# Strassen's scheme for groups 3 and 4 of three gate/up stages and four chunks of three down stages, with 1024-wide weight splits in gate/up

## The chip, the core and the metric

The kernel runs on one core of a Trainium2 chip, in one launch. The metric is the device time of that launch in microseconds (us), as a median of several executions. The core's engines are TensorE (matmuls into PSUM, which has 8 banks of 128 x 512 f32), VectorE, ScalarE and GpSimd for elementwise work, and SyncE (SP), from whose queue all loads and stores of this kernel are issued. Each engine runs its instructions in the order in which the program lists them, and waits on semaphores for what others have made.

## The reference

Two layers over 256 tokens of 1024 features, all in f32. Each layer is an FFN with a half step, a mixer (attention with a memory group), and a second FFN with a half step:

```python
def swiglu(h, w_gate, w_up, w_down):
    return (jax.nn.silu(h @ w_gate) * (h @ w_up)) @ w_down

for i in range(DEPTH):                                   # DEPTH = 2
    h = rmsnorm(x, ffn1_norm[i])
    x = x + 0.5 * swiglu(h, ffn1_w_gate[i], ffn1_w_up[i], ffn1_w_down[i])
    ...                                                  # mixer: x = x + concat(self_out, mem_out) @ W_out
    h = rmsnorm(x, ffn2_norm[i])
    x = x + 0.5 * swiglu(h, ffn2_w_gate[i], ffn2_w_up[i], ffn2_w_down[i])
```

`w_gate` and `w_up` are 1024 x 2816, `w_down` is 2816 x 1024. There are four FFNs: (0, 1), (0, 2), (1, 1) and (1, 2), by layer and place in the layer. The change touches the last three, and the width of the weight splits in all four.

## The kernel before

**Products.** An f32 product is made of three matmuls on values rounded to a shorter f32 form: with `hi` the rounded value and `lo` the rest, `dense` (L409) issues x_hi·w_hi (L416), x_hi·w_lo (L419) and x_lo·w_hi (L422) into the same bank. One `dense` multiplies a 128 x 128 block of activations by a 128 x 512 block of weights. Here it is called a product, and a product is three matmuls.

**Weights** come in chunks of four 128 x 512 blocks (1 MB). `loader` (L272) fetches a chunk into one of three `raw` tiles (NRAW); `split_hi` (L305) casts it to `hi` on ScalarE (L321), one instruction for each 512 columns; `split_lo` (L324) forms `lo` = raw - hi on VectorE (L340). `hi` and `lo` live in four tile pairs (NHL). A raw tile is free again once its splits are made, and a hi/lo pair once the products on it have run (`uses`). The three are "idle" threads of a planner.

**The planner.** The class `Flow` (L47) walks through the kernel with assumed durations and lists each engine's instructions in the order that its clock gives; the chip then runs them in that order, at its own speed. `dense` advances TensorE's clock and waits until its operands are due. Evacuations, sums and the like are threads that `yield` the time or the condition they wait for. Splits are put in order when the engine has at most 0.4 us of work before it, or when the chunk is the one that TensorE is at.

**A gate/up stage** (L640) has 11 groups of 256 columns of `w_gate` and the same 256 of `w_up`; a group has two chunks (upper and lower half of the 1024 rows), 8 products each: two token blocks `tb` times four row blocks. A group's two banks `gu` are evacuated by `evac` (L517): silu on ScalarE (L526), product with the up half on VectorE (L529), a block transpose (L537), then through DRAM (`hd`, `hr`, L543 and L548) to turn the blocks, and a split into `ht` (L557, L559), which the down stage takes as its stationary operand. Before the `ht` split is put in order, the thread waits 4.0 us of the planner's clock for the load of `hr`.

**A down stage** (L667) has 11 chunks, one for each group, accumulating in four `acc` banks. Chunks 0 to 7 run one after the other; chunks 8, 9 and 10 run together, ordered by token block and half, so that `finish` (L493) can add one quarter of the result to x while the next is computed. `finish` also transposes x for the next stage (`prep_half`, L450).

**Seven products for eight.** Three chunks of each down stage but the first (`SEVEN`, L362) already use Strassen's scheme (in Winograd's form): a chunk is a 2 x 2 grid of blocks and so is its activation operand; sums of blocks are formed on both sides and seven products take the place of eight. `split_lo` forms four sums of weights (`wsum`, L334), `seven_forms` (L564) four sums of activations from `hr`, `seven` (L591) issues the products, four of them into banks `m` of their own, and `seven_sums` (L602) adds these to x after the last such chunk: eight VectorE operations, which alternate with other work. Such a chunk needs two hi/lo pairs for its seven blocks. The forms of the third such chunk wait until the down stage has reached the second (`prog`).

Of the kernel before, what the change touches and what calls it, by code (L numbers as in the profile page):

```python
# [142 lines left out]
def kernel(  # L143
# [96 lines left out]
    class Chunk:  # L240
        def __init__(self, parts):
            self.parts = parts
            self.raw = self.hi = self.lo = None
            self.arrive = self.early = None
            self.seven = False
            self.hit = [None] * 7
            self.lot = [None] * 7
            self.tt = [None] * 4
            self.uses = 0

        def part(self, lo, q):

            t = (self.lo if lo else self.hi)
            if self.seven:
                t, q = t[q // 4], q % 4
            return t[:, q * 512:(q + 1) * 512]

    chunks = []
# [6 lines left out]
    def add_chunk(parts, uses=8):  # L265
        c = Chunk(parts)
        c.uses = uses
        c.index = len(chunks)
        chunks.append(c)
        return c  # L270

    def loader():  # L272
        for i, c in enumerate(chunks):
# [3 lines left out]
            c.block = lambda q, c=c: c.raw[:, q * 512:(q + 1) * 512] if not c.seven else c.raw[:, (0, 2, 3)[q] * 512:  # L277
                                                                                          (1, 3, 4)[q] * 512]
# [26 lines left out]
    def split_hi():  # L305
        for i, c in enumerate(chunks):
            n = 2 if c.seven else 1
            yield lambda: c.raw is not None and hl_left[0] >= n
            hl_left[0] -= n
            yield c.early or c.arrive  # L310
            c.hi, c.lo = ([whl.tile([P, 2048], F32R, tag=x, name=f"{x}{i}_{j}") for j in range(n)] for x in ("hi", "lo"))
            if not c.seven:
                c.hi, c.lo = c.hi[0], c.lo[0]
            for q in range(7 if c.seven else 4):
                if q == 2:
                    yield c.arrive
                if c.seven and q >= 3:
                    yield lambda: c.tt[q - 3] is not None
                    yield c.tt[q - 3]
                yield calm_a(i)  # L320
                nc.scalar.copy(out=c.part(0, q), in_=c.block(q))  # L321
                c.hit[q] = flow.act(512)

    def split_lo():  # L324
        for i, c in enumerate(chunks):
# [18 lines left out]
            if c.seven:  # L344
                g2.give(4)
# [1152 lines left out]
```

## Time and profile before

| | |
|---|---|
| median of three runs | 965.41 us (964.82 to 967.43) |
| the profiled execution's own time | 964.95 us |
| its span, first to last instruction | 963.2 us |
| TensorE matmuls, instructions | 4525 |
| VectorE instructions | 1569 |
| ScalarE instructions | 1215 |
| moved by DMA | 204.04 MB, mean 212 GB/s |

The span is what the profile shows; the 1.75 us between it and the execution's time lie before the first and after the last instruction. A page of the profile gives, in this order, the busy time of each engine, the same in 40 slices of the span, the DMA queues, the chain of work that ended last, and the costliest groups of instructions. PE is TensorE's matmuls and PEld its weight loads, DVE is VectorE, ACT is ScalarE, POOL is GpSimd. A group is named by its line, engine and operation, then by what it writes and reads in the program's names (`lo<-raw,hi`), shape, and count.

The four gate/up stages begin at 9.0, 317.5, 496.9 and 781.2 us, their down stages at 130.6, 437.7, 617.1 and 901.4 us.

### The profile page before, as it was taken

To read this page: it belongs to the slowest core of one execution; us is meant where nothing else is said; L and a number is where in the kernel's file an instruction comes from. 1 tells how busy PE (TensorE), PEld (TensorE's weight loads), DVE (VectorE), ACT (ScalarE), POOL (GpSimd) and SP (SyncE) were. 2 spreads that over 40 slices of the span, in tenths; PEclk is the share of its full clock that TensorE was granted. 3 is DMA by queue.
4 is the path that set the end of the run, shared out by engine and by line. 5 is a ranking of instruction groups with operands and counts; after the bars stand their busy time and mean duration, and the time that the engine had idled before them with its cause. 6 is when DMAs were issued, how large, how long until landed. Compare 5 with 4: busy or idle time off the path is not lost.

```text
span 963.2 us, 13464 instructions
## 1 busy us (share of the span) xinstructions
PE 954.8 (99%) x4525; PEld 783.9 (81%) x4525; DVE 745.0 (77%) x1569; ACT 567.9 (59%) x1215; POOL 60.5 (6%) x65
## 2 busy tenths in 40 slices
PE   8999999999999999999999999999999999999998
PEld 7888888888777888888888888888787788888886
DVE  6777777788777877759986775797989886776785
ACT  6655555666676655545645555565677765554551
POOL 0000000021210000000000000000343100000000
PEclk9999999999999999999999999999999999999999
DMA  8988877486525479766568777666641468777661
GB/s 282 328 267 285 250 263 246 145 272 208 176 88 175 154 224 284 235 229 205 184 208 254 247 245 220 212 202 219 207 143 44 134 196 283 232 254 225 215 190 44
DMA packets 169295, 204.04 MB, mean 212 GB/s; under 512 B 9673, under 2 KB 144394, under 8 KB 169226
## 3 DMA queue, kind: packets, MB, share of 16 engines
q1 hardware_dynamic: 169226, 203.18, 66.0%
q8 instruction: 35, 0.57, 0.2%
q14 instruction: 34, 0.28, 0.1%
HBM read 188.99 MB, written 14.16 MB: 211 GB/s over the span
## 4 chain that ended last, share of the span: by engine, by line
PE 94%; DVE 3%; ACT 1%; DMA 1%; SPq 0%; issue 0%; ACTq 0%
PE gu L422 17%; PE gu L416 17%; PE gu L419 17%; PE acc L416 9%; PE acc L422 9%; PE acc L419 9%; PE pj L422 3%; PE pj L416 3%; PE pj L419 3%; PE xtp L429 1%; PE ptp L429 1%; PE S L1139 1%; PE AV L1220 1%; PE m L422 1%; PE m L419 1%; PE m L416 1%
## 5 line engine op out<-in xcount | busy, mean ns | idle before, releaser
L340 DVE TENSOR_TENSOR lo<-raw,hi 128x512 fp32r<-128x512 f32 x647 | 413.7, 684 | 103.9 <-ACT hi L321 100.0
L321 ACT CAST hi<-raw 128x512 fp32r<-128x512 f32 x647 | 361.7, 618 | 219.0 <-PE gu L422 123.6
L422 PE MATMUL gu<-hi,xl 128*128 128x512 f32 x704 | 274.3, 390 | 0.0
L416 PE MATMUL gu<-hi,xh 128*128 128x512 f32 x704 | 274.1, 389 | 0.0
L419 PE MATMUL gu<-lo,xh 128*128 128x512 f32 x704 | 274.0, 389 | 0.0
L422 PEld LDWEIGHTS gu<-hi,xl 128*128 128x128 f32 x704 | 132.2, 188 | 27.4
L419 PEld LDWEIGHTS gu<-lo,xh 128*128 128x128 f32 x704 | 132.2, 188 | 27.3
L416 PEld LDWEIGHTS gu<-hi,xh 128*128 128x128 f32 x704 | 132.2, 188 | 27.3
L416 PE MATMUL acc<-hi,ht 128*128 128x512 f32 x280 | 109.6, 391 | 0.0
L422 PE MATMUL acc<-hi,ht 128*128 128x512 f32 x280 | 109.2, 390 | 0.0
L419 PE MATMUL acc<-lo,ht 128*128 128x512 f32 x280 | 109.1, 390 | 0.0
L422 PE MATMUL pj<-hi,xl 128*128 128x512 f32 x160 | 64.5, 403 | 0.0
L419 PE MATMUL pj<-lo,xh 128*128 128x512 f32 x160 | 63.6, 397 | 0.0
L416 PE MATMUL pj<-hi,xh 128*128 128x512 f32 x160 | 63.5, 397 | 0.0
L422 PEld LDWEIGHTS acc<-hi,ht 128*128 128x128 f32 x280 | 52.6, 188 | 11.0
L419 PEld LDWEIGHTS acc<-lo,ht 128*128 128x128 f32 x280 | 52.6, 188 | 10.7
L416 PEld LDWEIGHTS acc<-hi,ht 128*128 128x128 f32 x280 | 52.6, 188 | 10.7
L526 ACT ACTIVATE sil<-gu,xr 128x256 f32<-128x256 f32 x88 | 41.5, 472 | 28.6 <-PE gu L422 28.6
L559 DVE TENSOR_TENSOR ht<-hr,ht 128x512 fp32r<-128x512 f32 x35 | 24.1, 687 | 32.2 <-ACT ht L557 32.2
L529 DVE SCALAR_TENSOR_TENSOR h<-gu,xr,sil 128x256 f32<-128x256 f32 x88 | 42.2, 479 | 5.8 <-ACT sil L526 4.5
L557 ACT CAST ht<-hr 128x512 fp32r<-128x512 f32 x35 | 21.6, 618 | 41.9 <-DMA hr<-hd 41.8
L436 POOL TENSOR_TENSOR xr<-v,nhalf 128x1 f32<-128x1 f32 x12 | 8.4, 698 | 502.3 <-DVE v L434 502.3
(191 smaller groups left out, 1069.0 us busy)
## 6 DMA issues: line engine op xcount, KB each, us to landing
raw<-in_ffn_w_down_dram SPq DMA_DIRECT2D x176, 256.0 KB, 4.1
raw<-in_ffn_w_gate_dram SPq DMA_DIRECT2D x86, 512.0 KB, 4.3
raw<-in_ffn_w_up_dram SPq DMA_DIRECT2D x86, 512.0 KB, 5.5
raw<-in_w_in_dram SPq DMA_DIRECT2D x32, 512.0 KB, 4.1
hd<-hb SPq DMA_DIRECT2D x44, 256.0 KB, 2.3
hr<-hd SPq DMA_DIRECT2D x44, 256.0 KB, 5.3
raw<-in_w_out_dram SPq DMA_DIRECT2D x8, 1024.0 KB, 5.0
raw<-in_w_mem_kv_dram SPq DMA_DIRECT2D x4, 1024.0 KB, 5.4
```

The source lines that it names most:

```text
L321: nc.scalar.copy(out=c.part(0, q), in_=c.block(q))
L340: nc.vector.tensor_sub(c.part(1, q), c.block(q), c.part(0, q).bitcast(F32))
L416: nc.tensor.matmul(out=ps, lhsT=xh, rhs=wh, start=start, stop=False)
L419: nc.tensor.matmul(out=ps, lhsT=xh, rhs=wl, start=False, stop=False)
L422: nc.tensor.matmul(out=ps, lhsT=xl, rhs=wh, start=False, stop=stop)
L429: nc.tensor.transpose(out=dst, in_=src, identity=flip if flipped else ident)
L526: nc.scalar.activation(sil, ps[tb][:, 0:256], AF.Silu, scale=xt.r[tb])
L529: nc.vector.scalar_tensor_tensor(out=h, in0=ps[tb][:, 256:512], scalar=xt.r[tb], in1=sil, op0=ALU.mult, op1=ALU.mult)
L557: nc.scalar.copy(out=hi, in_=src)
L559: nc.vector.tensor_sub(lo, src, hi.bitcast(F32))
L1139: nc.tensor.matmul(out=ss[e][:, pr, :nk], lhsT=q[rows, pr, :], rhs=k[rows, pr, :], start=i == 0, stop=i == len(passes) - 1)
L1220: nc.tensor.matmul(out=av[64 * e:64 * e + 64, pr, :], lhsT=vsrc(kb, pr, e), rhs=pts[e][:, pr, kb, :], start=(kb == 0), stop=(kb == nb - 1))
```

## The change

1. In the last three FFNs, gate/up groups 3 and 4 are computed together. Their four chunks are a 2 x 2 grid of weights (row halves by groups), x is a 2 x 2 grid of activations (token blocks by row halves). `pair_items` forms four sums of weights (t1 to t4, four VectorE operations of 512 each), `pair_forms` four sums of x (eight VectorE operations, four casts), `product` issues seven products m1 to m7 of four `dense` each into a bank each, and `pair_sums` adds them to the four results, which `evac` then takes from SBUF. Blocks 11, 12, 22, 21 of the weights are loaded once; three of them (b11, b22, b21) are also used plainly. The seven items stand between plain chunks of groups 5 to 8, after groups 0 to 2.
2. Splits work on items with their own list of sources, no longer on chunks. A plain gate/up chunk is split by two instructions of 1024 columns on each engine instead of four of 512 (all four FFNs, the first two chunks of the kernel excepted).
3. `SEVEN` now has chunks 1, 3, 5 and 7 in each of the last three down stages.
4. `evac` waits 6.5 us of the planner's clock for `hr` instead of 4.0.
5. The forms of x need the f32 values `y` of the normalised, transposed x; `prep_half` keeps these four tiles until `pair_forms` has used them.

```diff
+    class Item:
+        def __init__(self, raws, uses=8, w=1):
+            self.raws, self.uses = raws, uses
...
+            self.n, self.frees, self.takes, self.gives = 1, 1, 0, 0
+            self.sums, self.t = [], []
+            self.index = len(items)
+            w = 1 if len(items) < 2 else w
+            self.units = [(self.own(q, w), q, w, None) for q in range(0, 4, w)]
+            items.append(self)
...
     def split_hi():
-        for i, c in enumerate(chunks):
-            n = 2 if c.seven else 1
-            yield lambda: c.raw is not None and hl_left[0] >= n
+        for i, it in enumerate(items):
+            yield lambda: hl_left[0] >= it.n and all(r.raw is not None for r in it.raws)
+            hl_left[0] -= it.n
+            yield max(r.early or r.arrive for r in it.raws)
...
+            for src, q, w, dep in it.units:
...
+                if dep is not None:
+                    yield lambda: it.st[dep] is not None
+                    yield it.st[dep]
                 yield calm_a(i)
-                nc.scalar.copy(out=c.part(0, q), in_=c.block(q))
+                nc.scalar.copy(out=it.part(0, q, w), in_=src())
...
     def split_lo():
+        for i, it in enumerate(items):
+            if it.sums:
+                yield lambda: all(r.raw is not None for r in it.raws) and g2.left >= it.takes + 2
+                yield max(r.arrive for r in it.raws)
+                it.t += [g2.take([P, 512], F32, "wsum") for _ in range(it.takes)]
+                for j, (x, y) in enumerate(it.sums):
+                    yield calm_v(i)
+                    nc.vector.tensor_sub(it.t[j], x(), y())
+                    it.st[j] = flow.dve(512)
+            for src, q, w, dep in it.units:
+                yield lambda: it.hit[q] is not None
+                yield it.hit[q]
+                yield calm_v(i)
+                nc.vector.tensor_sub(it.part(1, q, w), src(), it.part(0, q, w).bitcast(F32))
...
+            raw_left[0] += it.frees
+            g2.give(it.gives)
...
-    SEVEN = {(0, 1): (), (0, 2): (1, 4, 6), (1, 1): (1, 4, 6), (1, 2): (1, 4, 7)}
+    SEVEN = {(0, 1): (), (0, 2): (1, 3, 5, 7), (1, 1): (1, 3, 5, 7), (1, 2): (1, 3, 5, 7)}
+    PAIR = {(0, 1): None, (0, 2): 3, (1, 1): 3, (1, 2): 3}
...
+    def pair_items(raws):
+        r11, r12, r22, r21 = raws
+        def sums(need, x, y, held=None):
+            it = Item(need, 4)
+            it.t, it.takes = (held.t, 0) if held else ([], 4)
...
+            it.sums = [(at_(x, j), at_(y, j)) for j in range(4)]
+            it.units = [((lambda j=j: it.t[j]), j, 1, j) for j in range(4)]
+            return it
+        def plain(r, frees):
+            it = Item([r], 4, 2)
+            it.frees = frees
+            return it
...
+        def m5():
+            made["t1"] = sums([r12, r11], 0, 1)
+        def m7():
+            made["t3"] = sums([r22, r12], 0, 1)
+            made["t3"].gives = 4
+        def m6():
+            made["t2"] = sums([r22], 0, made["t1"], made["t1"])
+            made["t2"].frees = 0
...
+        def m4():
+            made["t4"] = sums([r21], 0, made["t2"], made["t2"])
+            made["t4"].gives = 4
...
     def plan_ffn(l, nm, wg, wu, wd):
+        work = [(g, c) for g in range(NG) for c in range(2)]
+        if pair is not None:
+            rest = [w for w in work if w[0] not in (pair, pair + 1)]
+            n = 2 * pair
+            p = iter(rest[n:])
+            work = rest[:n]
...
+            for x in ("11", "m1", "p", "12", "m5", "p", "22", "m7", "p", "m6", "p", "m3", "p", "p", "21", "m2", "p", "m4"):
+                work.append(next(p) if x == "p" else x)
+            work += list(p)
...
             hr = g2.take([P, 4, P], F32, "hr")
             nc.sync.dma_start(out=hr, in_=hd.rearrange("a i b x -> (i b) a x"))
-            yield flow.now + 4.0
+            yield flow.now + 6.5
...
+        def pair_forms():
+            yield lambda: len(xt.y) == 4 and g4.left >= 4
+            y = xt.y
+            fm = [g4.take([P, 2, 4, P], F32R, "xf") for _ in range(4)]
...
+            for j, o in ((0, (1, 1)), (2, (1, 0)), (1, (0, 0)), (3, (0, 1))):
+                yield lambda: flow.free["A"] <= flow.now + SLACK
+                nc.scalar.copy(out=fm[j][:, 0], in_=y[o])
+                yield flow.act(512)
+                yield lambda: flow.free["V"] <= flow.now + SLACK
+                nc.vector.tensor_sub(fm[j][:, 1], y[o], fm[j].bitcast(F32)[:, 0])
+                xt.ft[j] = flow.dve(512)
+                g2.give()
...
+        def pair_sums():
...
+            yield lambda: "m1" in mt
+            yield mt["m1"]
+            yield g2.has()
+            u = g2.take([P, 512], F32, "gu_u")
+            nc.scalar.copy(out=u, in_=pb["m1"])
...
+            yield lambda: "m6" in mt and "m7" in mt
+            yield mt["m6"]
+            yield g2.has(3)
+            u2, w, v = (g2.take([P, 512], F32, "gu_v") for _ in range(3))
+            plus(u2, u, pb["m6"])
+            plus(w, u2, pb["m5"])
+            t = plus(v, w, pb["m7"])
+            plus(u2, u2, pb["m7"])
...
+            for m, (g, tb), x in (("m3", (1, 0), w), ("m2", (0, 0), u), ("m4", (0, 1), u2)):
+                yield lambda: m in mt
+                yield mt[m]
+                t = plus(x, x, pb[m])
...
+        def product(m):
...
+            flow.until(banks.has())
+            pb[m] = bank("pair_" + m, (P, 512))
+            if m == "m1":
+                flow.spawn(pair_sums())
+                for e in range(2):
+                    flow.spawn(evac(pair + e, pps[e], pend[e], (g2, g2)))
+            for k in range(4):
...
+                t = dense(pb[m], fh, fl, ready, pit[name], k, k == 0, k == 3)
+            mt[m] = t
```

222 lines of the change are left out of this document (136 added, 86 removed).

## The prediction

> **What bounds the kernel now.** I read the page first, then TensorE's own waits, then the busy time of each engine in each stage. The page:
>
> ```profile
> span 963.2 us, 13464 instructions
> PE 954.8 (99%) x4525; PEld 783.9 (81%) x4525; DVE 745.0 (77%) x1569; ACT 567.9 (59%) x1215; POOL 60.5 (6%) x65
> ...
> PE   8999999999999999999999999999999999999998
> PEclk9999999999999999999999999999999999999999
> ...
> PE 94%; DVE 3%; ACT 1%; DMA 1%; SPq 0%; issue 0%; ACTq 0%
> ```
>
> TensorE is busy 99%, at full granted clock in every slice, and 94% of the chain that ended last is its work. Busy alone would not prove a bound, so its waits come next:
>
> ```profile
> PE warm L1425 <- POOL ident masks.py:199: 1.4, 1, 1.4
> PE xtp L429 <- DMA x<-in_x_dram: 1.1, 2, 0.9
> PE ptp L429 <- DVE pe L1266: 0.7, 2, 0.6
> PE acc L416 <- DVE oT L1127: 0.4, 1, 0.4
> PE qktp L429 <- DVE m L1045: 0.4, 1, 0.4
> PE qktp L429 <- ACT PT L1153: 0.4, 1, 0.4
> ```
>
> These six rows are the whole view (what waited for what: us, times, longest). They add up to 4.4 us, 2.5 of them in the opening (`warm`, `x`) and the rest in the attention part. In no FFN stage does a matmul wait for anything. The stages (gate/up, then down, of FFN 2 of layer 0, FFN 1 and FFN 2 of layer 1; columns: stretch, its length, busy time and instructions of each engine, clock, DMA):
>
> ```profile
> 317.50:437.70 120.20, 120.20 (x534) 99.52 (x533) 89.48 (x205) 67.24 (x133) 1.81 (x2) 1.00 0.72 228
> 437.70:496.90 59.20, 59.20 (x268) 49.01 (x267) 51.07 (x90) 33.14 (x64) 0.55 (x1) 1.00 0.64 204
> 496.90:617.10 120.20, 120.20 (x534) 99.52 (x533) 85.69 (x163) 66.54 (x130) 0.86 (x1) 1.00 0.76 237
> 617.10:676.30 59.20, 59.20 (x268) 49.00 (x267) 50.92 (x89) 34.54 (x66) 0.55 (x1) 1.00 0.63 204
> 781.20:901.40 120.20, 120.20 (x534) 99.55 (x533) 85.38 (x164) 67.35 (x133) 1.50 (x2) 1.00 0.72 228
> 901.40:959.30 57.90, 57.90 (x256) 47.66 (x254) 43.53 (x75) 25.68 (x49) 0.00 (x0) 1.00 0.47 150
> ```
>
> A gate/up stage has 22 chunks of 8 products of 3 matmuls, 528 in all: 120.2 / 528 = **0.2276 us a matmul**, 0.683 a product, 5.46 a plain chunk. So these stages last exactly as long as TensorE issues. VectorE is busy 85 to 89 us of 120 in gate/up (71 to 74%) and 51 of 59 in down (86%); ScalarE 56%. A matmul taken away is time saved as long as VectorE keeps up: that is the whole question.
>
> The Trainium skill ("Perfetto Trace Analysis", Identifying the Most-Contended Engine) calls matmul busy time a bad measure and judges by weight-load share, and VectorE by plain occupancy. By the page of the profile that is 81% against 77%, nearly level, which speaks for the rivals below. "TensorE: Matmul & The Clock Gate" (Wait — 56ns, not 53.3ns?) gives 0.2157 us for a warm 512-column matmul; the trace has 0.2276, and by the page the gain below would be 9.7 us.
>
> **The change, part by part.** *TensorE.* Groups 3 and 4 took 2 x 2 chunks x 8 = 32 products; now 7 of 4 = 28. That is 12 matmuls fewer in each of three stages, 36. Each of the three down stages turns one more chunk from 8 products into 7: 9 matmuls. 45 x 0.2276 = **10.2 us removed**. Nothing is added to TensorE.
>
> *VectorE and ScalarE.* Prices (by line and shape; after the bar busy time, mean ns, idle time before):
>
> ```profile
> L340 DVE TENSOR_TENSOR lo<-raw,hi 128x512 fp32r<-128x512 f32 x647 | 413.7, 684 | 103.9 <-ACT hi L321 100.0 <-DMA mr<-md 2.4 <-DMA raw<-in_ffn_w_down_dram 1.1
> L321 ACT CAST hi<-raw 128x512 fp32r<-128x512 f32 x647 | 361.7, 618 | 219.0 <-PE gu L422 123.6 <-issue 41.6 <-PE acc L422 21.4
> L559 DVE TENSOR_TENSOR ht<-hr,ht 128x512 fp32r<-128x512 f32 x35 | 24.1, 687 | 32.2 <-ACT ht L557 32.2
> L557 ACT CAST ht<-hr 128x512 fp32r<-128x512 f32 x35 | 21.6, 618 | 41.9 <-DMA hr<-hd 41.8
> L334 DVE TENSOR_TENSOR wsum<-raw,wsum 128x512 f32<-128x512 f32 x18 | 12.4, 688 | 0.3
> L611 DVE TENSOR_TENSOR msum<-msum,m 128x512 f32<-128x512 f32 x12 | 8.2, 682 | 0.7 <-DVE x L606 0.5
> L586 DVE TENSOR_TENSOR h<-sf,h 128x512 fp32r<-128x512 f32 x9 | 6.2, 686 | 0.3
> L586 DVE TENSOR_TENSOR h<-hr,h 128x256 fp32r<-128x256 f32 x9 | 3.6, 395 | 0.0
> L573 DVE TENSOR_TENSOR sf<-hr 128x128 f32<-128x128 f32 x18 | 5.2, 287 | 13.4 <-DMA hr<-hd 13.4
> L582 ACT CAST h<-hr 128x256 fp32r<-128x256 f32 x9 | 3.6, 402 | 0.0
> L529 DVE SCALAR_TENSOR_TENSOR h<-gu,xr,sil 128x256 f32<-128x256 f32 x88 | 42.2, 479 | 5.8 <-ACT sil L526 4.5
> L537 DVE STREAM_TRANSPOSE hb<-h 128x256 f32<-128x256 f32 x88 | 38.7, 440 | 1.0
> ```
>
> A 512-wide VectorE operation takes 0.684 us; in a row they overlap, so one costs 413.7 / 647 = 0.64. Wide splits (1024) are in no row. Two narrow ones cost 1.28 by that mean, which is one end (nothing saved); the other is 1.07, if everything over the streaming step of the L586 rows went (0.686 - 0.395 = 0.29 per 256, so 0.58 per 512 and some 0.1 of fixed part once instead of twice). I take 1.2, close to the 512-wide row: 0.686 + 0.58 less the overlap of 0.08 that four in 2.50 us show (below: (2.50 - 0.684) / 3 = 0.605 from one to the next). A gate/up stage then has 18 plain chunks and three plain pair blocks, 42 wide low splits, for 88 narrow: 50.4 for 56.3 us. Added: 4 weight sums of 4 operations and their 16 low splits, 32 x 0.64 = 20.5; eight operations on the forms of x, 5.3; seven sums of products with one operand in PSUM at 0.682, 4.8. Together +25: **110 of 117.5 us, 94%**, and 114 in the first of the three stages, which starts from 89.5. A down stage gains one seven-product chunk: 4 sums and 3 low splits, 4.4, and small-form work of about 2.5 for 0.69 saved: +6.2, so **57 of 58.5 us, 97%**; in the last down stage, which has nothing behind it to split, 50 of 57.2. ScalarE gains some 17 casts (10 us) and loses the pauses of 42 wide ones: near 62%, no bound; a wide cast should take 0.618 + 2 x (0.618 - 0.402) = 1.05.
>
> The longer wait before the `ht` cast is put in order (6.5 for 4.0) lets the 41.9 us in which ScalarE stood at L557 for DMA, and VectorE's 32.2 behind it at L559, go to other work. I count it as cover for the extra work, not as time saved: nobody on TensorE waited for it. If it fails, VectorE loses about 8 us in each gate/up stage.
>
> *Does the lead last in gate/up?* L321's idle time, 123.6 us for `gu`, shows the splits waiting for TensorE to free one of four hi/lo tiles: they run three items ahead, 3 x 5.46 minus the split, some 13 us. A Strassen item occupies a tile for 4 products only, 2.73 us, so three items ahead is 10.9 to 13.6 us there. I laid the work out by these durations (time 0 is the first product; a weight sum with its splits 5 us, a wide item 2.4, a group's evacuation 2 x (0.479 + 0.440) + 0.687 = 2.5). VectorE in order: 5b, whose tile is free at 0, with part of an evacuation, to 4.4; t3 to 9.4; 6a, whose load is asked for at 4.4 and lands near 10, to 13.4; t2 to 18.4; 1.8 of evacuation and 6b to 22.6; `ht` 0.7 and b22 to 25.7; product sums 2.7 and 7a to 31; 7b to 33.4; t4 to 44.5. TensorE asks for them at 10.9, 16.4, 19.1, 24.6, 27.3, 32.8, 35.5, 41 and 54.6. The least margin is 4.5 us. The change adds waits: the sums of t3 wait for block 22, whose load needs the tile of block 11, read last by t1's sums. It is asked for at about -2 and lands some 6 us later (gate 4.3 and up 5.5 after their issue, rows below), at 4, when VectorE comes to t3 anyway. Behind the sums stand the casts of t3 on ScalarE and, on both engines, the next evacuation; TensorE waits for neither before the margin is used up. SP issues the same loads and bytes, in another order. Forms of x are needed 41 us after the stage starts. **Cost taken: 0**; with the wait at L559 back, up to 3 us a stage.
>
> *Does it last in down?* Here the trace shows how little room there is at the end of the stage (VectorE; then TensorE's use of the same chunk, the last of the stage, by its low part):
>
> ```profile
> 619.85 2.45 DVE L340 TENSOR_TENSOR lo<-raw,hi 128x512 fp32r<-128x512 f32 x4
> 623.40 2.50 DVE L340 TENSOR_TENSOR lo<-raw,hi 128x512 fp32r<-128x512 f32 x4 [1.10 <-ACT hi L321]
> ...
> 659.25 0.68 DVE L340 TENSOR_TENSOR lo<-raw,hi 128x512 fp32r<-128x512 f32 x1
> 659.85 0.68 DVE L606 SCALAR_TENSOR_TENSOR x<-msum,x 128x512 f32<-128x512 f32 x1
> 660.45 3.09 DVE L340 TENSOR_TENSOR lo<-raw,hi 128x512 fp32r<-128x512 f32 x5
> ```
>
> ```profile
> 661.95 0.39 PE L416 MATMUL acc<-hi,ht 128*128 128x512 f32 x1
> 662.17 0.39 PE L419 MATMUL acc<-lo,ht 128*128 128x512 f32 x1
> ```
>
> The block of five at 660.45 begins with chunk 10's second quarter; its third ends at 660.45 + 0.605 + 0.684 = 661.74, and TensorE reads it at 662.17: 0.43 us to spare. Product sums (L606, L611) alternate with the splits one for one. Now sevens stand at 1, 3, 5, 7, and a seven needs two of the four tiles and 11 VectorE operations. Loading:
>
> ```profile
> raw<-in_ffn_w_down_dram SPq DMA_DIRECT2D x176, 256.0 KB, 4.1
> raw<-in_ffn_w_gate_dram SPq DMA_DIRECT2D x86, 512.0 KB, 4.3
> raw<-in_ffn_w_up_dram SPq DMA_DIRECT2D x86, 512.0 KB, 5.5
> 622.33 2.55 SPq L281 DMA_DIRECT2D raw<-in_ffn_w_down_dram  x4
> ```
>
> A chunk is issued in 2.55 us and its last part lands 4.1 after its issue, 6 us in all, from when the raw tile three chunks before is read. Time 0 is the stage's first product (617.3); VectorE ends chunk 2 at 5.0 (row 619.85). Then, at 0.605 an operation: sums of 3 to 7.4, its splits to 11.7; chunk 4 to 14.1; sums of 5 to 16.6; `ht` 17.3; the forms of 5 and 7, released together, 22.3; splits of 5 to 26.6; 6 to 29.0; sums and splits of 7 to 35.8; 8 to 38.2; 9 to 40.6. TensorE begins 3 at 15.7, 5 at 25.9, 6 at 30.7, 7 at 36.2, 8 at 41.0, 9 at 42.3, 10 at 43.7: margins of 3 to 4 us at each first quarter from 5 on. Chunk 10's load, asked for when 7's raw part has been read (33.4), lands near 39.5; its third quarter is needed at 44.4. With three low splits and two or three product sums ahead, 41.1 + 1.9 + 1.6 = 44.6. So 0.2 late, up to 3 us with VectorE's usual pauses, or not late at all if the order falls well. I take **0.6 us a stage, 1.8 in all**. The extra seven saves 0.68 a stage: in down the change is about a wash.
>
> **Sum.** 964.95 (the profiled execution; span 963.2 and 1.75 around it) - 10.2 + 1.8 = 956.5. That execution lies 0.46 below the median of the three runs, 965.41, so against the median 956.9.
>
> **Rivals.**
> 1. *No stall at all*: VectorE keeps up everywhere, 964.95 - 10.2 = 954.7, or 955.2 by the median. For it: the margins in gate/up. Against: 0.43 us at the end of down.
> 2. *Down stages become VectorE's*: 57 of 58.5 us leaves nothing for pauses; the trace's 51 of 59.2 had 8 us of them. If 2 to 4 us of those return at chunks 9 and 10 in each stage, 6 to 12 us come back: 961 to 967 (the last stage, at 50 of 57.2, pays least).
> 3. *Slower: gate/up becomes VectorE's*. From the first product to t4 TensorE has 57 us of work, VectorE about 66 (10 wide items 24, four weight sums 20, forms 5.3, product sums 4.8, five evacuations 12.5). I let 9.6 us be done ahead and 10 lie outside. If that lead is not there, because tiles freed at 2.73 us instead of 5.46 do not let it build, each stage waits 9 us: 3 x 9 - 10.2 = +17, 982 us. It decides from where VectorE's lead at t3 or t2 falls below the 5 us that a weight sum takes. By the rule of the Trainium skill named above, with VectorE at 94% of a stage and weight loads at 81%, this would be the expected end.
> 4. *It doesn't do what it says*: the matmul count stays, 965. Products and chunks are counted out in the diff; hardly possible.
>
> **How the numbers follow.** Forecast (954.7 to 960, some 1 to 4 us of stalls) 0.50; rival 1 0.18; rival 2 0.19, a third of it below 962.5; rival 3 0.12, a part of it near 970; rival 4 0.01. A difference under 0.3% (2.9 us) is no difference that can be told here. Faster: 0.50 + 0.18 + 0.06 = 0.74; the same 0.14; slower 0.12. The range goes from 954.2 (nothing waits, and the runs' spread of 0.6 below) to 964.5, which takes in the greater part of rival 2 and leaves out about 0.18.
>
> **What would show it.** TensorE's 512-wide matmuls fall by 45 and gate/up stages 2, 3, 4 last 117.5 us each; a longer stage with TensorE waiting for `lo` (VectorE) is rival 3. The down stages: idle of TensorE for VectorE's `lo` at chunk 10, near 0.6 us; 2 or more is rival 2. L557's idle for `hr` should fall from 41.9 to near 0; the wide splits' mean should be near 1.05 on ScalarE and 1.27 on VectorE. The prediction is wrong if VectorE, still under 97% in each stage, makes TensorE wait by its order of work rather than by its amount.

## The result, and the profile after

The changed kernel takes 974.72 us (median; 973.84 to 975.66), against 965.19 us for the kernel before on the same chip: a ratio of 1.0091, 95% interval 1.0074 to 1.0108. It is slower by 9.5 us where the prediction had 956.9 and a range up to 964.5.

The page of the changed kernel (engine, busy time, instructions; slices of the span; the chain that ended last):

```profile
span 972.6 us, 13283 instructions
PE 953.1 (98%) x4480; PEld 780.0 (80%) x4480; DVE 822.2 (85%) x1571; ACT 585.0 (60%) x1115; POOL 65.3 (7%) x65
...
PE   8999999999999999999899999998999999999997
...
PEclk8999999999999999999989999999999999999999
...
PE 58%; DVE 22%; DMA 12%; issue 3%; ACT 3%; SPq 2%; POOL 0%; DVEq 0%; ACTq 0%
```

There are 4480 matmuls instead of 4525: the 45 are gone. But two slices in the middle (the 20th and the 28th of 40) are no longer full for TensorE, the slice right behind the first of them is short of clock, as is the very first, and the chain, which was 94% TensorE, is now 58% TensorE, 22% VectorE and 12% DMA: in places VectorE sets the end. The view of TensorE's waits and the table by stage say where (the second gate/up stage, 321.44 to 438.87; then the three down stages; columns as in the prediction; windows rounded to a tenth of a us):

```profile
PE acc L499 <- DVE lo L344: 9.3, 6, 2.5
PE xtp L509 <- DMA x<-in_x_dram: 3.1, 1, 3.1
321.40:438.90 117.50, 117.50 (x522) 97.27 (x521) 105.60 (x173) 70.59 (x108) 2.39 (x2) 1.00 0.72 230
438.90:505.10 66.20, 62.20 (x265) 50.05 (x264) 59.35 (x113) 36.54 (x69) 0.08 (x1) 0.95 0.58 188
622.60:686.60 64.00, 60.89 (x266) 49.36 (x265) 59.26 (x118) 38.82 (x75) 0.89 (x1) 0.97 0.60 195
908.70:968.80 60.10, 57.87 (x253) 46.96 (x251) 49.65 (x90) 28.77 (x55) 0.00 (x0) 1.00 0.46 149
```

The gate/up stage lasts 117.4 us, 2.8 less than before, and TensorE is busy in all of it; the other two do the same. That is 8.3 us won, as the prediction had it. The down stages last 66.3, 64.0 and 60.1 us in place of 59.2, 59.2 and 57.9: 14.0 us lost. At full issue they would be 58.5, 58.5 and 57.3 (one of the kernels below reaches these), so some 16 us in them are stall, of which the waits of `acc` for `lo` are 9.3. Most of the rest lies where the granted clock fell: it is 0.95 and 0.97 in the first two.

8.3 won and 14.0 lost make 5.7; the profiled execution is 9.4 us longer. The remaining 3.7 lie in the opening, where a load of `x` landed late (3.1 us in the waits above) and the clock was 0.87 up to 30 us. Whether that belongs to the change is the last experiment's question.

The end of a down stage, VectorE first, then TensorE (start, length, engine, line, tiles, count, idle before):

```profile
477.63 4.90 DVE L344 TENSOR_TENSOR lo<-raw,hi 128x512 fp32r<-128x512 f32 x8
483.10 0.69 DVE L690 SCALAR_TENSOR_TENSOR x<-msum,x 128x512 f32<-128x512 f32 x1 [0.57 <-ACT msum L701]
484.25 0.69 DVE L695 TENSOR_TENSOR msum<-msum,m 128x512 f32<-128x512 f32 x1 [0.46 <-DVE x L690]
484.85 0.68 DVE L344 TENSOR_TENSOR lo<-raw,hi 128x512 fp32r<-128x512 f32 x1
485.45 0.68 DVE L695 TENSOR_TENSOR msum<-msum,m 128x512 f32<-128x512 f32 x1
486.17 0.69 DVE L690 SCALAR_TENSOR_TENSOR x<-msum,x 128x512 f32<-128x512 f32 x1
486.78 1.89 DVE L344 TENSOR_TENSOR lo<-raw,hi 128x512 fp32r<-128x512 f32 x3
```

```profile
485.59 0.50 PE L499 MATMUL acc<-lo,ht 128*128 128x512 f32 x1 [2.45 <-DVE lo L344]
...
488.12 0.80 PE L499 MATMUL acc<-lo,ht 128*128 128x512 f32 x1 [1.55 <-DVE lo L344]
...
489.14 0.63 PE L496 MATMUL acc<-hi,ht 128*128 128x512 f32 x1
489.57 0.63 PE L499 MATMUL acc<-lo,ht 128*128 128x512 f32 x1
```

The eight at 477.63 are the splits of chunks 8 and 9. Then come two operations on the sums of products (L690, L695; ScalarE copies a product before the first), the first quarter of chunk 10 (484.85), two more sums, and only then its other quarters. TensorE waits twice, for the first quarter and for the third: 2.45 and 1.55 us. After that its matmuls start 0.43 us apart (489.14 to 489.57, and so on to 493.41) where they are 0.2276 apart elsewhere. The clock of that stretch:

```profile
488.20:494.90 6.70, 6.70 (x20) 5.24 (x21) 5.56 (x8) 0.00 (x0) 0.00 (x0) 0.57 0.55 165
```

The granted clock is 0.57 here. The Trainium skill ("TensorE: Matmul & The Clock Gate", What's actually happening) says that TensorE drops to half rate after an idle window of about 3.4 us. The 0.43 us against 0.2276 agree roughly with half rate; each of the two idle stretches here, 2.45 and 1.55 us, is shorter than that window (more on this at the end). Of this stage's 7.7 us over full issue, 4.4 are the two waits (starts 2.95 and 1.95 us apart, less 0.2276 each) and some 3.2 the clock.

Why is VectorE late? Look half a stage earlier, at the queue of SyncE, then at ScalarE and at VectorE behind it:

```profile
440.21 7.90 SPq L288 DMA_DIRECT2D raw<-in_ffn_w_down_dram  x8
448.15 0.58 SPq L627 DMA_DIRECT2D hd<-hb  x1
452.15 0.37 SPq L632 DMA_DIRECT2D hr<-hd  x1
```

```profile
449.31 0.62 ACT L326 CAST hi<-raw 128x512 fp32r<-128x512 f32 x1 [0.38 <-ACT hi L326]
454.92 0.62 ACT L641 CAST ht<-hr 128x512 fp32r<-128x512 f32 x1 [4.99 <-DMA hr<-hd]
455.44 1.66 ACT L326 CAST hi<-raw 128x512 fp32r<-128x512 f32 x3
457.44 0.63 DVE L670 TENSOR_TENSOR h<-hr,h 128x256 fp32r<-128x256 f32 x2 [1.06 <-ACT h L666]
```

The same store, load and cast in the kernel before, whose stage begins at 437.7:

```profile
440.71 0.34 SPq L543 DMA_DIRECT2D hd<-hb  x1
445.74 0.54 SPq L548 DMA_DIRECT2D hr<-hd  x1
449.86 0.62 ACT L557 CAST ht<-hr 128x512 fp32r<-128x512 f32 x1 [2.17 <-DMA hr<-hd]
```

In the kernel after, the transpose of the last group (`hb`) ends 5.5 us into the stage, at 444.4. Its way through DRAM (`hd`, then `hr`) is issued by SP, whose queue is at that time in a run of eight weight loads. Four alone take 2.55 us to issue; these eight take 7.90, since one of them waits for VectorE. SP's waits in that stretch (us, times, longest):

```profile
SPq L288 <- DVE ht L643: 2.8, 1, 2.8
```

2 x 2.55 + 2.8 = 7.9. So `hd` goes out at 448.15 and `hr` at 452.15. ScalarE comes to the `ht` cast at 449.93, stands still for 4.99 us (this idle wait is called its stand below), and the casts queued behind it stand with it. VectorE, which has work in hand, waits 1.06 us of that, for the cast of a form `h`. In the three down stages this last stand is 4.99, 4.91 and 3.83 us, in the kernel before 2.17, 2.59 and 2.84. The kernel as a whole shows the same by line and shape (busy, mean ns, idle before):

```profile
L641 ACT CAST ht<-hr 128x512 fp32r<-128x512 f32 x32 | 19.8, 618 | 56.9 <-DMA hr<-hd 56.8
L643 DVE TENSOR_TENSOR ht<-hr,ht 128x512 fp32r<-128x512 f32 x32 | 21.9, 684 | 21.8 <-ACT ht L641 21.7
L326 ACT CAST hi<-raw 128x1024 fp32r<-128x1024 f32 x166 | 168.9, 1048 | 95.0 <-PE gu L502 38.6 <-DMA raw<-in_ffn_w_up_dram 37.7 <-issue 9.9
L344 DVE TENSOR_TENSOR lo<-raw,hi 128x1024 fp32r<-128x1024 f32 x166 | 199.1, 1218 | 28.4 <-ACT hi L326 27.9 <-DMA raw<-in_ffn_w_gate_dram 0.3
```

The stand of ScalarE for `hr` has grown from 41.9 to 56.9 us. A wide cast costs what was foreseen, 1.05 us; a wide low split 1.22, a little less than the 1.27 foreseen.

### The profile page after: what moved, and what is told of

Read it like the earlier page. It is cut to its first block, busy times and chain, and to the rows that moved or that the text cites. A ratio compares the mean times of both kernels' runs of the same rounds, so it can differ in the third digit from the quotient of the medians.

```text
span 972.6 us, 13283 instructions
## 1 busy us (share of the span) xinstructions
PE 953.1 (98%) x4480; PEld 780.0 (80%) x4480; DVE 822.2 (85%) x1571; ACT 585.0 (60%) x1115; POOL 65.3 (7%) x65
## 4 chain that ended last, share of the span: by engine, by line
PE 58%; DVE 22%; DMA 12%; issue 3%; ACT 3%; SPq 2%; POOL 0%; DVEq 0%; ACTq 0%
DVE lo L344 12%; PE gu L496 8%; PE gu L502 8%; PE gu L499 8%; PE acc L499 5%; PE acc L496 5%; PE acc L502 5%; DMA raw<-in_ffn_w_up_dram 5%; DMA hd<-hb 3%; DVE wsum L338 3%; PE pj L502 3%; PE pj L496 3%; PE pj L499 3%; ACT hi L326 2%; DMA hr<-hd 2%
## 5 line engine op out<-in xcount | busy, mean ns | idle before, releaser
L326 ACT CAST hi<-raw 128x512 fp32r<-128x512 f32 (+1 forms) x466 | 337.1, 771 | 150.1 <-PE gu L502 44.6
L344 DVE TENSOR_TENSOR lo<-raw,hi 128x512 fp32r<-128x512 f32 (+1 forms) x466 | 392.7, 877 | 39.9 <-ACT hi L326 39.4
L502 PE MATMUL gu<-hi,xl 128*128 128x512 f32 x608 | 237.7, 391 | 0.0
L496 PE MATMUL gu<-hi,xh 128*128 128x512 f32 x608 | 237.6, 391 | 0.0
L499 PE MATMUL gu<-lo,xh 128*128 128x512 f32 x608 | 237.4, 390 | 0.0
L499 PEld LDWEIGHTS gu<-lo,xh 128*128 128x128 f32 x608 | 114.6, 188 | 23.8
L496 PEld LDWEIGHTS gu<-hi,xh 128*128 128x128 f32 x608 | 114.7, 189 | 23.6
L502 PEld LDWEIGHTS gu<-hi,xl 128*128 128x128 f32 x608 | 114.6, 188 | 23.7
L326 ACT CAST hi<-wsum 128x512 fp32r<-128x512 f32 x96 | 56.5, 620 | 40.2 <-DVE wsum L338 37.6
L344 DVE TENSOR_TENSOR lo<-wsum,hi 128x512 fp32r<-128x512 f32 x96 | 60.6, 685 | 0.0
L641 ACT CAST ht<-hr 128x512 fp32r<-128x512 f32 x32 | 19.8, 618 | 56.9 <-DMA hr<-hd 56.8
```

The source lines that it names most:

```text
L326: nc.scalar.copy(out=it.part(0, q, w), in_=src())
L344: nc.vector.tensor_sub(it.part(1, q, w), src(), it.part(0, q, w).bitcast(F32))
L496: nc.tensor.matmul(out=ps, lhsT=xh, rhs=wh, start=start, stop=False)
L499: nc.tensor.matmul(out=ps, lhsT=xh, rhs=wl, start=False, stop=False)
L502: nc.tensor.matmul(out=ps, lhsT=xl, rhs=wh, start=False, stop=stop)
L641: nc.scalar.copy(out=hi, in_=src)
```

## The experiments

The theory that these runs led to has two parts. **The late `hr`**: that of the last group comes late, ScalarE stands for it with casts behind it, and VectorE comes to the splits of chunk 8 some 2 to 3 us behind (2.4 against e9 below, 3 against the prediction's list). **The sums between the splits**: the sums of products, put between the splits of the last chunk, turn the remaining lateness into two waits of TensorE, and these into half clock. The rivals: **the amount** (VectorE's work with a fourth seven, 97% of a stage, is too much, whatever its order); **gate/up** (groups 3 and 4 there disturb the down stages); **the wide splits** (they hold the narrow ones up).

All times here are medians; the ratio is against the kernel before in the same session. The stages are those of the profiled execution, counted from the first product of a down stage to that of the next stage (the third to its last product).

| kernel | us (lowest to highest) | ratio (95%) | down stages, us |
|---|---|---|---|
| after | 974.72 (973.84–975.66) | 1.0091 (1.0074–1.0108) | 66.3, 64.0, 60.1 |
| e1 three sevens | 961.05 (958.78–963.55) | 0.9947 (0.9927–0.9968) | 59.3, 62.2, 58.0 |
| e2 only the four sevens | 986.22 (985.98–987.03) | 1.0210 (1.0195–1.0226) | 64.7, 64.5, 66.0 |
| e3 sums late | 963.06 (959.49–965.69) | 0.9971 (0.9956–0.9986) | 60.3, 60.5, 60.7 |
| e4 wait 4.0 | 985.58 (984.09–987.44) | 1.0203 (1.0183–1.0223) | 66.5, 67.3, 67.9 |
| e5 other queue | 960.73 (958.23–962.00) | 0.9941 (0.9920–0.9962) | 60.9, 60.0, 57.8 |
| e6 wait 9.0 | 960.42 (959.48–972.97) | 0.9961 (0.9933–0.9989) | 59.9, 60.5, 59.1 |
| e7 three sevens, sums late | 957.61 (957.43–960.10) | 0.9918 (0.9898–0.9939) | 60.3, 59.3, 58.0 |
| e8 three sevens, narrow | 958.34 (957.61–960.84) | 0.9924 (0.9903–0.9946) | 59.3, 59.7, 58.2 |
| e9 sums late, other queue | 955.73 (955.14–959.07) | 0.9904 (0.9886–0.9921) | 58.6, 58.6, 57.3 |
| e10 sums late, wait 9.0 | 957.63 (956.78–961.38) | 0.9915 (0.9900–0.9931) | 58.6, 59.5, 57.3 |
| e11 as e7, other queue | 958.62 (957.61–959.23) | 0.9927 (0.9913–0.9940) | 59.3, 59.3, 58.0 |
| e12 after, once more | 973.48 (970.08–975.99) | 1.0077 (1.0060–1.0095) | 64.2, 65.4, 59.8 |

Several of these times lie outside all that was expected: e2 is 6 us slower, e5 and e6 are 3 and 6 us faster, and e3, e8, e10 and e11 are off by 0.1 to 2 us. One of the ten executions of e6 took 972.97 us; it wasn't profiled.

### Which part of the change costs it: e1, e2, e8

e1 is the kernel after with the chunks of seven as before; e8 is e1 with splits of one quarter; e2 is the kernel before with nothing but the four sevens.

```diff
-    SEVEN = {(0, 1): (), (0, 2): (1, 3, 5, 7), (1, 1): (1, 3, 5, 7), (1, 2): (1, 3, 5, 7)}
+    SEVEN = {(0, 1): (), (0, 2): (1, 4, 6), (1, 1): (1, 4, 6), (1, 2): (1, 4, 7)}
```

> The changed kernel with the seven-product chunks put back to where they were (1, 4, 6; 1, 4, 6; 1, 4, 7); pairs and wide splits kept. If the down stages alone lose the time (the fourth seven-product chunk is too much for VectorE), the three gate/up stages stay at 117.4 us, the down stages return to 59.2, 59.2 and 58.0, and the time is 965 - 8.2 = 957 us, or 961 if the 3.9 us lost in the first 25 us come again. If instead the loss in the down stages is a debt that the fuller gate/up stages leave behind, they stay above 61 us and the time is 963 to 968.

```diff
-    SEVEN = {(0, 1): (), (0, 2): (1, 4, 6), (1, 1): (1, 4, 6), (1, 2): (1, 4, 7)}
+    SEVEN = {(0, 1): (), (0, 2): (1, 3, 5, 7), (1, 1): (1, 3, 5, 7), (1, 2): (1, 3, 5, 7)}
```

> The kernel of before with the seven-product chunks at 1, 3, 5, 7 and nothing else. If the fourth such chunk alone is too much for VectorE, the down stages last 62 to 66 us each of the first two and 60 the third, and the time is 972 to 980 us. If the loss needs the fuller gate/up stages too, the down stages last 59 to 60 and the time is 963 to 967.

```diff
-            it = Item([r], 4, 2)
+            it = Item([r], 4, 1)
...
-                gu[w] = add_chunk(parts(*w), 8, 2)
+                gu[w] = add_chunk(parts(*w), 8, 1)
```

> Three seven-product chunks and the pairs, but splits of 512 columns everywhere (961.05 with wide ones). By my estimate of 1.2 us for a wide low split against 1.28 for two narrow ones, VectorE gains 3 us a gate/up stage from wide splits, and at 94% with 4.5 us of margin it does without: within 2 us of 961. If the wide splits are what makes the pairs affordable, TensorE now waits for lo in the gate/up stages and the time is 965 or more.

TensorE's wait for `lo` in e2, which has no group by Strassen in gate/up and no wide split:

```profile
PE acc L419 <- DVE lo L340: 13.2, 9, 1.9
```

The fourth seven alone costs 21 us (986.22 - 965.28), 18.7 of them in the three down stages of the profiled execution, so neither the gate/up groups nor the wide splits are needed for the loss. e2 has the old wait of 4.0, like e4 below, which takes nearly the same time (985.58). Groups 3 and 4, with the wait of 6.5 and nothing else (e8), bring 7.4 us (965.76 - 958.34) of the 8.2 that 36 matmuls are worth. In e8 the last cast of a down stage stands 4.6, 3.9 and 3.4 us, nearly as long as in the kernel after, and the sums stand between the splits, yet TensorE waits only 0.2 us for `lo` there: with three sevens there is room for both. The wide splits bring little either way: they spare VectorE 2 us in a gate/up stage (105.9 against 107.9 us busy in the second) and make nothing faster, 961.05 us (e1) against 958.34 (e8), with runs that overlap. e1 is not quite free of stall: 62.2 in its second down stage, with two waits of TensorE for `lo` (2.4 us).

### The order of the sums, and the stand for `hr`: e3, e4, e5, e6

e3 lets the sums of products begin only when the last chunk's splits are placed (and has the stage's last addition to `x` and the rope's users wait for what then comes later):

```diff
             yield t
+            yield lambda: dn[NG - 1].lot[3] is not None
             yield g2.has(2)
             u, w = (g2.take([P, 512], F32, "msum") for _ in range(2))
```

> The changed kernel with the product sums of a down stage put in order only after the last chunk's splits (and the addition to x waiting for them), the same work in another order. If order makes TensorE wait (sums between the splits of chunk 10), the two waits in each down stage fall from 4.4, 3.5 and 2.5 us to below 1 and the time is near 965 us. If amount makes it wait (chunk 10's load asked for too late because VectorE is behind), the first wait stays at 1 to 2.5 us, only the second (1.6 us) goes, and the time is 969 to 972.

e4 and e6 change the planner's wait before the `ht` cast, and e5 the engine that issues `hd` and `hr`:

```diff
-            yield flow.now + 6.5
+            yield flow.now + 4.0
```

> The changed kernel with the old wait of 4.0 us of the planner's clock before the ht cast. If the longer wait gives VectorE and ScalarE time back as the prediction had it, this is slower than the changed kernel by 2 us or more, with more idle time of ScalarE for hr than 57 us. If the wait for hr now comes from the store that stands behind a weight load on SP's queue, no choice of this number helps: within 2 us of the changed kernel.

```diff
-            nc.sync.dma_start(out=hd.rearrange("a i b x -> (a i) (b x)"), in_=hb.rearrange("p b t f j -> p (b t f j)"))
+            nc.gpsimd.dma_start(out=hd.rearrange("a i b x -> (a i) (b x)"), in_=hb.rearrange("p b t f j -> p (b t f j)"))
...
-            nc.sync.dma_start(out=hr, in_=hd.rearrange("a i b x -> (i b) a x"))
+            nc.gpsimd.dma_start(out=hr, in_=hd.rearrange("a i b x -> (i b) a x"))
```

> The changed kernel with the store hd and the load hr of each group issued from GpSimd's queue instead of SP's, so that no weight load stands before them. If these transfers are late because they queue behind weight loads that wait for a tile, ScalarE's idle for hr falls from 57 us to below 20, the waits of TensorE in the down stages shrink by 2 us or more a stage, and the time is 964 to 969. If they are late because DMA is slow or shared, the idle stays above 45 us and the time stays at 973 to 977.

```diff
-            yield flow.now + 6.5
+            yield flow.now + 9.0
```

> The changed kernel with a wait of 9.0 us of the planner's clock before the ht cast, where 4.0 gave 985.6 and 6.5 gives 974.7. If the cast's place in ScalarE's order is what costs (it stands at the head of the queue and waits for hr, and the hi casts behind it wait with it), another 2.5 us of it give back 3 to 9 us: 966 to 972. If VectorE's amount of work sets the down stages, nothing comes of it: 973 to 977.

ScalarE's waits for `hr` (us, times, longest) in e4, and below in e6:

```profile
ACT ht L641 <- DMA hr<-hd: 87.7, 27, 9.0
```

```profile
ACT ht L641 <- DMA hr<-hd: 9.8, 7, 2.2
```

With 4.0, 6.5 and 9.0 the stand is 87.7, 56.8 and 9.8 us and the time 985.58, 974.72 and 960.42: the stand in three doses (the last cast of a down stage stands 7.7 to 9.0, 3.8 to 5.0 and 0.9 to 2.2 us). (The planner lays out everything anew at each value, so the dose isn't pure: in the first down stage `hd` goes out 0.0, 3.8 and 1.4 us after `hb`. With 4.0 it is the early cast and not a late `hd` that makes the stand.) e5 changes the issuing engine alone, and TensorE, VectorE and ScalarE run the same instructions in the same order as in the kernel after: 14 us gained. `hd` follows `hb` after 0.3 us, and ScalarE's stand in the three down stages falls from 5.0, 4.9 and 3.8 us to 1.4, 0.9 and 0.7. But over the whole kernel it hardly falls, 53.8 us after 56.8, where under 20 had been expected. So the total of that row is a bad gauge: most of it lies in gate/up, where TensorE waits for nothing.

e3 leaves the stand as it was or longer (59.0 us; 5.5, 5.5 and 6.6 in the down stages) and gains 11.7 us all the same, so the sums between the splits are a cause of their own. The two gains overlap: 14.0 and 11.7 make 25.7, and both edits at once bring 19.0 (e9). TensorE's waits in e3:

```profile
PE acc L499 <- DVE lo L344: 3.9, 7, 2.5
```

At chunk 10 they are about 0.2 us each. The longest, 2.5 us, comes 24 us into the third down stage, after the stand of 6.6.

Either edit alone leaves 5 to 8 us over the 955 that nothing but TensorE's issue would give: in e5 and e6 most stages have one more wait, of up to 1.6 us, at chunk 10, with sums among its splits. Up to here the amount could still have been the reason for the rest.

### Both causes taken away: e9, e10, and the same with three sevens: e7, e11

> The kernel after with both edits at once: product sums only after the last chunk's splits, and hd and hr issued from GpSimd's queue. Theory (two causes, ScalarE's stand for hr and the sums between the splits, and nothing else): down stages at 58.6, 58.6 and 57.3 us (256 and 250 matmuls or so at 0.2276), no wait of TensorE for lo of 0.5 us or more, time 2 us under the three-sevens kernel with late sums (957.61): 955 to 957. Rival (VectorE's amount of work, 97% of the stage, is what is short with four sevens): one wait of 1 to 2 us at chunk 10 is left in each of the first two down stages, and the time stays at 959 to 962, as with either edit alone (963.06 and 960.73).

> The kernel after with the product sums after the last chunk's splits and the wait before the ht cast at 9.0 instead of 6.5; hd and hr stay on SP's queue. Theory (what counts is that ScalarE does not stand for hr, however that is brought about): as with the other queue, 955 to 957, down stages at 58.6, 58.6 and 57.3, no wait of TensorE for lo at chunk 10. Rival (the amount of VectorE's work): 959 to 962 with one wait of 1 to 2 us left in two stages. A second rival (the later ht delays the forms of chunks 5 and 7, so that TensorE waits in the middle of the stage): waits for x or ht at chunk 5 or 7, 960 or more.

> The pairs and wide splits with three seven-product chunks as in the kernel before, and the product sums after the last chunk's splits. If both order and amount are what the changed kernel lost by, the two waits (1.7 and 1.0 us) left in FFN 1 of layer 1 go too, every down stage lasts 58 to 60 us, and the time is 956.5 to 959. If the sums, put late, now delay the next stage's first operands, it is 960 to 963.

> The three-sevens kernel with late sums (957.61) with hd and hr issued from GpSimd's queue. Theory: TensorE waited for nothing in its down stages already, so the earlier hr gives nothing that can be told: 956.5 to 958.5, down stages 59.25, 59.25 and 58.0. Rival (the stand for hr still costs somewhere in gate/up or at the stage ends): 954 to 956.

e9, some lines of its page and its three down stages:

```profile
PE 945.5 (99%) x4480; PEld 776.0 (81%) x4480; DVE 820.4 (86%) x1571; ACT 584.0 (61%) x1115; POOL 121.6 (13%) x153
...
PEclk9999999999999999999999999999999999999999
```

```profile
435.78:494.32 58.54, 58.54 (x265) 48.48 (x264) 56.47 (x105) 34.97 (x64) 1.31 (x2) 1.00 0.65 207
612.52:671.07 58.55, 58.55 (x265) 48.47 (x264) 57.05 (x115) 37.66 (x74) 1.49 (x3) 1.00 0.60 197
892.56:949.83 57.27, 57.27 (x253) 47.10 (x251) 50.21 (x91) 29.42 (x57) 1.30 (x2) 1.00 0.45 152
```

The down stages last as long as TensorE issues, at full clock; the view of its waits has no wait for `lo`. VectorE does as much as in the kernel after (820.4 us in all, against 822.2), 56.5 us of 58.5 in the first of them (96%). So the amount fits: what cost the time was when the cast of `hr` could run, and where the sums stood. The fourth seven is a condition, since it takes the room away in which both were harmless. From e3 to e9 the three engines run the same instructions in the same order, so the 7.3 us between them (963.06 - 955.73) come from the queue of `hd` and `hr` alone. ScalarE's stand and the end of the stage, in e9:

```profile
440.54 0.56 POOL L629 DMA_DIRECT2D hd<-hb  x1 [7.48 <-DVE hb L623]
445.00 0.75 POOL L634 DMA_DIRECT2D hr<-hd  x1 [3.90 <-DMA hd<-hb]
```

```profile
448.51 0.62 ACT L643 CAST ht<-hr 128x512 fp32r<-128x512 f32 x1 [1.67 <-DMA hr<-hd]
```

```profile
472.13 7.31 DVE L344 TENSOR_TENSOR lo<-raw,hi 128x512 fp32r<-128x512 f32 x12
479.35 0.69 DVE L692 SCALAR_TENSOR_TENSOR x<-msum,x 128x512 f32<-128x512 f32 x1
```

`hd` is issued 4.8 us into the stage (9.25 in the kernel after), ScalarE stands 1.67 us instead of 4.99, and VectorE begins chunk 8's splits at 472.13, 36.4 us into the stage, and goes through all twelve of chunks 8, 9 and 10 by 479.44, 43.7 us into it; then the sums begin. In the kernel after the last three of those splits began at 486.78 and ended 49.8 us into it.

e10 takes most of the stand away by the other means and comes to 957.63, 0.6 above what was expected of it: its second down stage keeps 0.9 us, a wait of 0.8 for `x`. It also settles a rival of e5 and e9: on SP's queue the weight loads stand behind an `hr` that waits for its `hd` to land (7.0 us in the first down stage of the kernel after), and GpSimd's queue takes that away too. e10 leaves 4.4 us of it there, and its first down stage lasts 58.6 all the same. e7 and e11 show what the fourth seven is worth once it is free: 957.61 and 958.62 with three, 955.73 with four, 1.9 and 2.9 us for the 2.0 that nine matmuls make (9 x 0.2276). In e11 the earlier `hr` brings nothing, as expected: with three sevens and late sums TensorE waited for no `lo` in down, although e7 has the largest stand of those at 6.5 (69.9 us). (The 60.3 in e7's first down stage is a wait of 0.9 us for `x`, which the late sums bring late. In e3, e9 and e10 the gate/up stage of FFN 1 of layer 1 lasts 118.2 us instead of 117.4, with a wait of 0.4 for its first operands: a small price of the same kind.)

e9 beats both kernels: 955.73, ratio 0.9904 (0.9886 to 0.9921).

### The opening: e12

> The kernel after once more, unchanged, for the part of its loss that no stage of the FFNs holds: in the profiled execution the gate/up stages gave 8.3 us and the three down stages took 14.0, and the other 3.7 us lie in the opening, where a load of x landed late and the clock was at half for a while. Theory (the opening comes and goes with the landing of x and has nothing to do with the change): the down stages stand at 64 to 66.5, 64 and 60 again, the first gate/up product comes at 8.7 to 10.5 us, and the time is 970 to 975. Rival (the opening is the change's): the first gate/up product at 11 us again, with the clock under 0.9 up to 30 us, and 974 to 975.5.

The same code as the changed kernel; the profiled run took 970.93 us. Its opening and its first two down stages:

```profile
9.41:30.00 20.59, 20.57 (x97) 16.80 (x96) 18.16 (x28) 15.68 (x27) 3.20 (x2) 1.00 1.00 321
435.15:499.33 64.18, 60.71 (x265) 49.42 (x264) 58.95 (x112) 36.26 (x68) 0.12 (x1) 0.97 0.61 193
616.76:682.20 65.44, 62.29 (x265) 50.20 (x264) 58.99 (x117) 38.54 (x75) 0.88 (x1) 0.95 0.60 189
```

The same stretch of the opening in the first profiled execution of this code:

```profile
11.04:30.00 18.96, 18.96 (x79) 15.56 (x78) 13.87 (x22) 12.24 (x21) 2.90 (x2) 0.87 0.84 268
```

The first product came at 9.41 us instead of 11.04, and the clock up to 30 us was full instead of 0.87; the down stages lost 13.1 us. SP issues the opening's loads in the same order in all kernels, and e10's profiled execution had the late opening as well (10.94; 961.38, against its median of 957.63). So the 3.7 us come and go with the landing of `x`; why it lands late at times is open. How often it did in the unprofiled executions isn't known.

## Why the prediction was wrong

**Right.** 45 matmuls at 0.2276 us: gate/up stages of 117.4 us each, no wait in them, as "cost taken: 0" had it. That is rival 3 refuted: VectorE was busy 105.6 to 106.5 us of a stage, less than the 110 to 114 that I had summed up (the wide low split at 1.22 in a row with 0.08 of overlap is 48 us of the 50.4 foreseen; part of the rope's set-up work also slid on into the down stages). The price of a wide cast was 1.05 us, as estimated; of a wide low split 1.22, where 1.27 had been estimated.

**The step that failed** is "The longer wait before the `ht` cast is put in order (6.5 for 4.0) lets the 41.9 us in which ScalarE stood at L557 for DMA, and VectorE's 32.2 behind it at L559, go to other work." The idle time of that line was to fall to near 0 and rose to 56.9 (VectorE's behind it did fall, from 32.2 to 21.8). Most of this row lies in gate/up, where it costs nothing; the casts that count are the last of each down stage. I had taken the landing of `hr` as fixed and moved only the cast. But `hb` ends 2.5 us later (5.5 us into the first of these stages, 3.0 before), since ScalarE and VectorE come to the last group's evacuation later (its second silu starts 1.9 us into the stage, 0.8 before), and `hd` stands in SP's queue behind eight loads, one of which waits for VectorE: 9.25 us into the stage instead of 3.0. For gate/up I had said that SP "issues the same loads and bytes, in another order", and gave that order no price, there or in down. With e5 alone, which takes `hd` and `hr` out of it, 14 us come back.

**The size that followed from it**: 0.6 us of stall in a down stage, measured 7.7, 5.4 and 2.8. My list of VectorE's work had chunk 7's splits end at 35.8 us and chunk 10's third quarter at 44.6, on the silent condition that each cast is there when VectorE wants it. In the kernel after, chunk 7's end at 477.71, 38.8 us into the stage, 3 us behind. Held against e9, 1.0 us of them is there at the stage's start; VectorE's last wait before it was for the `ht` cast of an earlier group (0.45 us, with ScalarE standing 1.71 for that `hr`), but that this brought the 1.0 us isn't shown. 1.3 come with the stand of 4.99 (VectorE's own wait is 1.06). The other 0.6 are in e9 too; set-up operations for the rope run in the stage, which the list had left out. The condition is nearly met in e9, and there the list holds: chunk 8 begins at 36.4 (35.8 in the list), and TensorE waits for no `lo`. Two more terms were too small or missing. I gave the sums between the splits of chunk 10 1.6 us; they took 2.3 (482.53 to 484.85) and 1.3 (485.53 to 486.78), since one waits for the other and for ScalarE's copy. And a wait of TensorE was priced at its own length, not with the half clock behind it, 3.2 and some 2 us in two stages.

**Rivals.** Rival 2 had the place right (VectorE's `lo` at chunks 9 and 10) with 6 to 12 us to come back; it was 14, and its reason, too much work for the stage, is what e9 refutes. Its ceiling was set by the pauses of the kernel before. The last line of what would make it wrong is what happened: VectorE, busy 90% of the first down stage (59.4 of 66.3 us), makes TensorE wait by its order and not by its amount. Part of it was another queue's order: e5 keeps VectorE's order and changes only where `hd` and `hr` are issued. It should have had a price there and not stood as a remark.

## What to carry to other kernels

Before a wait on a DMA is taken as covered, ask when that DMA can be *issued* (what stands before it in its queue) and what stands behind the waiting instruction: here a cast that stood 5 us held up all casts behind it, and through them VectorE and TensorE. Work that nobody waits for, such as the sums of products, belongs behind the last item on which the bound engine waits; between the splits it was harmless with 8 us of slack in the stage (59.2 - 51) and cost some 12 us, over three stages, with 2 (58.5 - 56.5) and a late start. And a short wait of TensorE is priced with the clock that may fall after it.

## What the hardware showed unexpectedly

- Two idles of TensorE of about 1.5 us each, with three matmuls between them, were enough for some 3 us of half clock (second down stage: starts 1.95 and 1.96 us apart, then 0.427 from 671.6 to 674.5; clock 0.97). The Trainium skill ("TensorE: Matmul & The Clock Gate", Why this matters for your kernels) advises against idle gaps of over 3 us; here neither gap alone was as long. Single waits of up to 1.6 us (e5, e6) and one of 2.5 (e3) left the clock at full, and so did waits of 0.7 and 1.6 us in the third down stage. No length follows from these runs: in e2 two waits of 1.1 and 1.6 us at chunk 10 were followed by half clock in the first down stage, and two of the same lengths in the second were not.
- The engine that issues a DMA mattered by 14 us. The Trainium skill ("DMA: Bandwidth & Descriptors", Issuing engines are not separate DMA queues) says that issuing on several engines saves only the sequencer's time to start a DMA, usually small. Here the start of a transfer was what counted: in e9 `hd` was started 4.5 us earlier in the stage than in the kernel after (4.76 against 9.25; 1.0 of this because `hb` was ready earlier), since on SP it stood behind eight loads that took 7.90 us, 5.1 of them to issue and 2.8 a wait for VectorE.
